# Long convolution of a hybrid encoder layer: short convolutions loaded two blocks ahead, the output transform split over two phases, the branch's first products beside the last spectra's turns

## The chip, the cores and the metric

The kernel runs on one core of one Trainium2 chip. Its time is the device time of the program in microseconds, the median of three runs.

## The reference, cut to what matters

One encoder layer, float32, 2048 positions of 1024 channels. An input projection feeds two mixers (a gated long convolution and a scan with a delta-rule state), their results are projected, gated, merged and normalised, and a feed-forward block follows. The change lies in the long-convolution mixer and in the first products of the merge behind it.

```python
def hyena_mixer(u, conv_w, conv_b, ..., skip):
    u = short_conv3(u, conv_w, conv_b)            # 3 taps over positions, 1536 channels
    v, x1, x2 = jnp.split(u, 3, axis=-1)          # 512 channels each
    h = hyena_filters(L, ...)
    z = x1 * long_conv(v, h[:, 0, 0], h[:, 0, 1], sk[0])    # by FFT of length 2L
    z = x2 * long_conv(z, h[:, 1, 0], h[:, 1, 1], sk[1])
    return z
...
y_h = hyena_mixer(u_h, ...) @ w_hy_out
y_r = rwkv_mixer(u_r, ...) @ w_rw_out
mix = (g_h * y_h + g_r * y_r) @ w_o
```

## The kernel before, in words

The 512 channels of the mixer are four blocks c = 0..3 of 128. For each block there are three rows of short convolution: v (row c), x1 (row 4 + c) and x2 (row 8 + c), each 128 channels by 2048 positions, computed in four blocks of 512 positions. The long convolutions are matrix products: a forward transform, a product with the filter's spectrum, an inverse transform. In order, the parts are:

- `shorts` (lines 1147 to 1183) is a generator; each `next` does one block of a row: SP loads block k+1 into one of two buffers `cu` (the inner `given`, line 1155, issued at the start of convolution k), ScalarE scales block k (line 1173), VectorE adds the two other taps (lines 1174 and 1179). The order of the rows is 0, 4, then 1, 5, 8, 2, 6, 9, 3, 7, 10, 11. Their results lie in two row buffers, X0 and X1. The row of block 0 is made in `open` (line 1115), near the end of the scan (`chain`), which ends with `output(*late.pop())` (line 1083) and leftover pieces of the scan and of the filters.
- `turn` (1267) transposes 4 x 128 positions on TensorE, and ScalarE copies them; `fwd` (1274) is a quarter of the forward transform, with two copies to `U` on ScalarE; `flips` (1284) gives a tile `V` and `piece(q)`, a 32x32-block transpose on VectorE (line 1289) of a quarter. The next step on TensorE reads all four quarters.
- `product` (1320), numbered 0 to 7, two for each channel block, has eight steps q. In each, TensorE makes `pz` from `V` (1295), VectorE multiplies it by the spectrum (1337 and 1338), TensorE makes `pz` of the spectrum two steps ahead (`load`, 1308, whose halves SP swaps with four small DMAs `rg<-rg`, line 1315) and turns the step before back (`back`, `pq`, 1328 and 1329). `extras[q]` are further works hung on step q: convolutions, pieces of transposes, turns. `self.upto` pulls pieces of the filter's transform (`pf`, `pg`), the filler of the stage; `goals` sets how far each step pulls. The spectra `Vf` are fetched by SP from DRAM (`given`, 1301).
- `inverse` (1353) is a quarter of the inverse transform (`po`). After an even product, the inner phase multiplies it by x1 into `z` (1443) and goes forward again; after an odd one, `finish` (1362) transposes it back to channels (`pv`, 1368, on TensorE), multiplies by x2 (the gate, 1370, VectorE) and stores the row to `yhd`.
- `ready` (1484) hangs on product 7 what the merge's first products need: eight weight tiles of the other branch, loaded and split into two parts each (ScalarE casts, VectorE subtracts, lines 197 and 198), gate values, the branch's rows `yrd` (`branch`, 1527). `right` (1521) is one such product, 12 matmuls of 128x256, with its gate on VectorE.

In the scan only TensorE's order is by hand, and a planner orders the other engines. In `hyena` the orders of TensorE, ScalarE, VectorE and SP are as written, so each engine and SP's queue take their work strictly in program order. The stage after product 2c, before the change, for c > 0, and the inner phase after it:

```python
piece(0); piece(1)
finish(c - 1, VQ2, x2, lambda q: piece(q + 1) if q in (1, 2) else None)
self.upto(min(self.pieces + 3, 32 * HT))
for q in range(6):
    if q < 4: p = inverse(VQ, q); tt(out=z[...], in0=p, in1=x1[...], op=ALU.mult)
    if q > 1: fwd(z, U, q - 2)
```

Of the kernel before, what the change touches and what calls it, by code (L numbers as in the profile page):

```python
# [189 lines left out]
class Layer:  # L190
# [432 lines left out]
    def chain(self):  # L623
# [3 lines left out]
        with tc.tile_pool(name="ch", bufs=1, reuse_waits="tile") as s, tc.tile_pool(name="chp", bufs=1, space=PSUM, reuse_waits="tile") as ps:  # L627
# [405 lines left out]
            with tc.manual_schedule(engines={mybir.EngineType.PE}):  # L1033
# [113 lines left out]
    def shorts(self):  # L1147
# [7 lines left out]
        def given(k):  # L1155
            ct, b = seq[k]
# [7 lines left out]
            return u  # L1164

        u = given(0)
        for k, (ct, b) in enumerate(seq):
            nxt = given(k + 1) if k + 1 < len(seq) else None
            if b == 0:
                o = self.cm.tile([P, L], F32, name="co", tag="X1" if ct == HT or ct >= 2 * HT else "X0")  # L1170
# [11 lines left out]
            u = nxt  # L1182
# [71 lines left out]
    def hyena(self):  # L1254
# [4 lines left out]
        with tc.tile_pool(name="hy", bufs=1, reuse_waits="tile") as s, tc.tile_pool(name="hyp", bufs=2, space=PSUM, reuse_waits="tile") as ps, \  # L1259
# [3 lines left out]
            def zt(name):  # L1263
                return s.tile([P, 16, P], F32, name=name, tag=name, bufs=1)

# [95 lines left out]

            def finish(c, Q, x2, beside):
                xv = x2.rearrange("p (a b) -> p b a", b=32)

                def back(q, v):
                    p = ps.tile([P, 4, P], F32, name="pv", tag="pq")
                    for j in range(4):
                        nc.tensor.transpose(p[:, j], v[:, j], self.ident)
                    w = xv[:, 8 * q:8 * q + 8]
                    tt(out=w, in0=p.rearrange("p a (b c) -> p (a b) c", b=2), in1=w, op=ALU.mult)  # L1370

                last = None
                for q in range(5):
                    if q < 4:
                        p = inverse(Q, q)
                        v = self.next("A")
                        nc.scalar.copy(v, p)
                    if q > 0:
                        back(q - 1, last)
                    beside(q)  # L1380
                    last = v
                if c == HT - 1:
                    self.yh = self.wp.tile([P, 2, TB], F32R, name="yh", tag="ev", bufs=2)
                    self.split(self.yh[:, 0], self.yh[:, 1], x2[:, 0:TB])
                nc.sync.dma_start(self.yhd[c], x2)
# [7 lines left out]
            def conv():  # L1393
                next(self.conv)
# [10 lines left out]
            x1, o = zt("x1"), self.convs.pop(HT)  # L1405
            Vz, piece = flips(U)
            for q in range(4):
# [3 lines left out]
                turn(o, x1, q)  # L1411
                self.upto(32 if q == 3 else min(32, self.pieces + 2))
            post, held = None, None
            for c in range(HT):
# [3 lines left out]
                if post:  # L1418
                    VQ2, piece2 = held
                    for q in range(4):  # L1420
# [3 lines left out]
                if more:  # L1424
                    for q in range(4, 8):
                        extras[q].append(conv)
# [3 lines left out]
                if post:  # L1430
                    x2 = self.convs.pop(2 * HT + c - 1)
                    piece(0)
                    piece(1)
                    finish(c - 1, VQ2, x2, lambda q: piece(q + 1) if q in (1, 2) else None)
# [373 lines left out]
```

## Time and profile before

| | us |
|---|---|
| median of three runs (4058.3 to 4072.2) | 4059.35 |
| the profiled execution | 4057.78 |
| its span, first to last instruction | 4056.0 |
| PE busy | 3851.7 |
| VectorE busy | 2350.6 |
| ScalarE busy | 1459.1 |

The profile is one execution. PE is TensorE's matmuls and PEld its weight loads; each float32 matmul shows as two records, a matmul of the rounded type as one. A busy PE at a granted clock of 0.5 does half the work. The long convolution lies between 1633 and 2205 us of the span; projection and scan lie before it, merge and feed-forward behind it.

### The profile page before, as it was taken

The page shows a single profiled execution, that of the slowest core. Times are in us where ns is not written, and L with a number is a line of the kernel's source. Part 1 is how long each engine was busy: PE and PEld are TensorE (multiplying, and loading weights), DVE is VectorE, ACT ScalarE, POOL GpSimd, SP SyncE. Part 2 cuts the span into 40 slices and gives each one's busy share as a digit, 9 for nine tenths or more (in the row PEclk, how much of TensorE's full clock was granted, in tenths as well). Part 3 has the DMA queues.
Part 4 walks back from the last instruction along what each step waited for, and adds up shares of the span by engine and source line. Part 5 has one row for each costly group of instructions (what it writes and reads, how often), then busy time and mean ns, then how long its engine had stood idle before and what let it go on. Part 6 is the DMA issues. An engine that isn't in the chain of part 4 may idle for free.

```text
span 4056.0 us, 64933 instructions
## 1 busy us (share of the span) xinstructions
PE 3851.7 (95%) x26152; PEld 3151.0 (78%) x26152; DVE 2350.6 (58%) x3734; ACT 1459.1 (36%) x2853; POOL 93.0 (2%) x139
## 2 busy tenths in 40 slices
PE   8999999899999998888987999999999999999998
PEld 6766557777777776788887899788888878888887
DVE  5456884665667774476665656544444464444444
ACT  3345662333335576555543323311111141111113
POOL 0000001111110100000000000000000000000000
PEclk9999999999999999899998999999999999999999
DMA  4566877677777766444454533411111133111111
GB/s 137 175 169 174 218 208 238 197 210 206 218 208 210 218 188 193 130 117 120 120 133 147 164 115 123 161 59 50 47 47 47 47 111 97 47 47 47 47 47 42
DMA packets 426564, 535.43 MB, mean 132 GB/s; under 512 B 137412, under 2 KB 305869, under 8 KB 423509
## 3 DMA queue, kind: packets, MB, share of 16 engines
q1 hardware_dynamic: 365847, 459.91, 38.7%
q10 hardware_dynamic: 54528, 54.59, 4.3%
q0 software_dynamic: 5888, 16.78, 1.6%
q8 instruction: 206, 3.38, 0.3%
q14 instruction: 95, 0.78, 0.1%
HBM read 369.52 MB, written 144.70 MB: 127 GB/s over the span
## 4 chain that ended last, share of the span: by engine, by line
PE 50%; DMA 3%; DVE 3%; ACT 2%; SPq 1%; issue 1%; DVEq 0%; ACTq 0%
PE pg L202 4%; PE pg L204 4%; PE pu L202 4%; PE pg L203 4%; PE pu L203 4%; PE pu L204 4%; PE pd L202 4%; PE pd L204 4%; PE pd L203 4%; PE pz L1295 2%; PE pm L204 1%; PE pm L202 1%; PE pm L203 1%; DMA cu<-ud 1%; PE po L202 1%; PE po L203 1%
## 5 line engine op out<-in xcount | busy, mean ns | idle before, releaser
L202 PE MATMUL acc<-xh,wh 128*128 128x512 f32 x1376 | 577.9, 420 | 10.4 <-ACT xh L197 10.4
L203 PE MATMUL acc<-xl,wh 128*128 128x512 f32 x1376 | 548.9, 399 | 9.4 <-DVE xl L198 9.4
L204 PE MATMUL acc<-xh,wl 128*128 128x512 f32 x1376 | 549.7, 399 | 0.5 <-DVE wl L198 0.5
L1745 DVE TENSOR_TENSOR acc<-pd,acc 128x1024 f32<-128x1024 f32 x320 | 387.5, 1221 | 70.8 <-PE pd L204 64.9
L197 ACT CAST fwh<-raw 128x1024 fp32r<-128x1024 f32 x132 | 138.5, 1049 | 704.2 <-PE pg L203 488.4
L202 PEld LDWEIGHTS acc<-xh,wh 128*128 128x128 f32 x1376 | 260.9, 190 | 123.5 <-issue 47.2
L1773 DVE TENSOR_TENSOR h<-pu,sg 128x512 f32<-128x512 f32 x88 | 60.8, 691 | 491.3 <-PE pu L204 485.3
L203 PEld LDWEIGHTS acc<-xl,wh 128*128 128x128 f32 x1376 | 261.4, 190 | 72.7 <-DVE xl L198 12.8
L204 PEld LDWEIGHTS acc<-xh,wl 128*128 128x128 f32 x1376 | 261.4, 190 | 63.8 <-DVE wl L198 1.0
L202 PE MATMUL pd<-fwh,hh 128*128 128x512 f32 x704 | 277.0, 394 | 1.8 <-DVE acc L1743 1.4
L202 PE MATMUL pg<-fxh,fwh 128*128 128x512 f32 x704 | 276.7, 393 | 0.2 <-DVE fxl L1660 0.2
L202 PE MATMUL pu<-fxh,fwh 128*128 128x512 f32 x704 | 276.3, 393 | 0.4 <-ACT fxh L1659 0.4
L204 PE MATMUL pg<-fxh,fwl 128*128 128x512 f32 x704 | 276.4, 393 | 0.0
L204 PE MATMUL pu<-fxh,fwl 128*128 128x512 f32 x704 | 276.1, 392 | 0.0
L203 PE MATMUL pu<-fxl,fwh 128*128 128x512 f32 x704 | 276.1, 392 | 0.0
L203 PE MATMUL pg<-fxl,fwh 128*128 128x512 f32 x704 | 275.9, 392 | 0.0
L204 PE MATMUL pd<-fwh,hl 128*128 128x512 f32 x704 | 275.1, 391 | 0.0
L203 PE MATMUL pd<-fwl,hh 128*128 128x512 f32 x704 | 274.5, 390 | 0.0
L198 DVE TENSOR_TENSOR fwl<-raw,fwh 128x1024 fp32r<-128x1024 f32 x132 | 161.1, 1221 | 165.8 <-ACT fwh L197 162.0
L198 DVE TENSOR_TENSOR wl<-wraw,wh 128x512 fp32r<-128x512 f32 (+1 forms) x217 | 169.7, 790 | 146.4 <-ACT wh L197 145.5
L197 ACT CAST wh<-wraw 128x512 fp32r<-128x512 f32 (+1 forms) x217 | 150.4, 704 | 232.0 <-PE acc L203 196.0
L202 PEld LDWEIGHTS pd<-fwh,hh 128*128 128x128 f32 x704 | 132.0, 187 | 40.6 <-DVE acc L1745 5.4
(288 smaller groups left out, 7545.9 us busy)
## 6 DMA issues: line engine op xcount, KB each, us to landing
wraw<-in_w_in SPq DMA_DIRECT2D x130, 512.0 KB, 4.6
ABp<-ABd SPq DMA_DIRECT2D x64, 512.0 KB, 5.6
raw<-in_fg SPq DMA_DIRECT2D x44, 512.0 KB, 3.4
raw<-in_fu SPq DMA_DIRECT2D x44, 512.0 KB, 3.5
raw<-in_fd SPq DMA_DIRECT2D x44, 512.0 KB, 3.5
ud<-ev ACTq DMA_DIRECT2D x84, 256.0 KB, 3.6
ABd<-AB SPq DMA_DIRECT2D x32, 512.0 KB, 5.3
gated<-ev SPq DMA_DIRECT2D x64, 256.0 KB, 3.4
```

Source lines behind the costliest of these rows:

```text
L197: nc.scalar.copy(hi, src)
L198: nc.vector.tensor_tensor(out=lo, in0=src, in1=hi.bitcast(F32), op=ALU.subtract)
L202: mm(ps, ah, bh, start=start, stop=False)
L203: mm(ps, ah, bl, start=False, stop=False)
L204: mm(ps, al, bh, start=False, stop=stop)
L1295: mm(p[:, j], Mc[:, 0 if 4 * q + j == 0 else 3], v[:, j], start=True, stop=True)
L1745: tt(out=acc[t], in0=pf, in1=acc[t], op=ALU.add)
L1773: tt(out=h, in0=put, in1=sg, op=ALU.mult)
```

## The change

- The loads of the short convolutions are issued two blocks ahead: two at the start, then that of block k+2 after convolution k, into the buffer that it has just read. The last row goes to X0 instead of X1.
- The row x1 of block 0 (four convolutions) is made at the end of the scan instead of beside the first turns. The other convolutions keep their number; within odd products they stand at steps 2, 4, 5, 6, 7, 7, and in even ones at 2, 3 (from c = 1 on) and 4 to 7. The last row moves from product 7 to product 6.
- The turns of x1 for the next block move from the last two steps of the odd product to the first four of the next even one; the pieces of transposes that hang on products move one step later.
- The output transform (`finish`) becomes `result`, `back` and `gate`. After an even product VectorE does its four pieces in a row; TensorE does the four inverses of the output and two backward turns. Gates and the other two turns go between the steps of the inner phase.
- Filler between an even product and the inner phase: six pieces for c = 0 and two otherwise, instead of three.
- The branch weights are loaded and split in product 6 instead of product 7. The branch's rows, its gate values and their `Tanh` come after the last block's transposes of `z`, into the row buffers `x1` and `z`, and three of the seven first products stand before product 7; four stand beside the last transposes. Product 7 has no extras. What `rest` loaded comes after product 7.

```diff
@@ chain
                 output(*late.pop())
+                self.x1 = self.short(HT)
@@ shorts
+        rows = {HT: "X1", 3 * HT - 1: "X0"}
...
-        u = given(0)
+        given(0)
+        given(1)
         for k, (ct, b) in enumerate(seq):
-            nxt = given(k + 1) if k + 1 < len(seq) else None
+            u = self.cus[k % 2]
...
-            u = nxt
+            given(k + 2)
             yield
@@ hyena
+            def result(Q, q):
+                p = inverse(Q, q)
+                v = self.next("AB"[q % 2])
+                nc.scalar.copy(v, p)
+                return v
+            def back(v):
+                p = ps.tile([P, 4, P], F32, name="pv", tag="pq")
+                for j in range(4):
+                    nc.tensor.transpose(p[:, j], v[:, j], self.ident)
+                return p
+            def gate(p, x2, q):
+                w = x2.rearrange("p (a b) -> p b a", b=32)[:, 8 * q:8 * q + 8]
+                tt(out=w, in0=p.rearrange("p a (b c) -> p (a b) c", b=2), in1=w, op=ALU.mult)
...
                 if q < 4:
                     turn(self.z0, z, q)
-                    conv()
...
-                turn(o, x1, q)
-                self.upto(32 if q == 3 else min(32, self.pieces + 2))
+                turn(self.x1, x1, q)
+                self.upto(32 if q == 3 else min(32, self.pieces + 3))
...
+                if c:
+                    VQ2, piece2 = held
+                    x1 = zt("x1")
                     for q in range(4):
-                        extras[q].append(lambda q=q: piece2(q))
-                    for q in (1, 3):
-                        extras[q].append(conv)
+                        extras[q].append(lambda q=q: turn(o1, x1, q))
+                        extras[q + 1].append(lambda q=q: piece2(q))
+                    extras[2].append(conv)
+                    extras[3].append(conv)
+                for q in range(4, 8):
+                    extras[q].append(conv)
+                if not more:
+                    self.ready(extras)
...
                 for q in range(4):
                     piece(q)
+                if c:
+                    x2 = self.convs.pop(2 * HT + c - 1)
+                    vs = [result(VQ2, q) for q in range(4)]
+                    ws = [back(vs[q]) for q in range(2)]
+                self.upto(min(self.pieces + 2 if c else self.pieces + 6, 32 * HT))
...
+                inner(0)
+                inner(1)
+                gated(0)
+                fwd(z, U, 0)
+                inner(2)
+                gated(1)
+                fwd(z, U, 1)
+                more_back(2)
+                inner(3)
+                gated(2)
+                fwd(z, U, 2)
+                more_back(3)
+                fwd(z, U, 3)
+                Vz, piece = flips(U)
+                gated(3)
+                if c:
+                    nc.sync.dma_start(self.yhd[c - 1], x2)
+                for q in range(4):
+                    piece(q)
...
+                else:
+                    self.inputs()
+                    for dt in range(3):
+                        self.right(ps, dt)
...
-                    for q in (1, 3, 4, 5, 6, 7):
+                    for q in (2, 4, 5, 6, 7, 7):
                         extras[q].append(conv)
...
+            self.outputs()
             for q in range(4):
                 piece(q)
-                self.right(ps, q)
+                self.right(ps, 3 + q)
+            for q in range(6):
+                if q < 4:
+                    vs.append(result(VQ, q))
+                if 0 < q < 5:
+                    ws.append(back(vs[q - 1]))
+                    gate(ws[q - 1], x2, q - 1)
@@ ready
+        extras[1].append(first)
+        for dt, q in enumerate((3, 4, 5, 5, 6, 6, 7, 7)):
+            extras[q].append(lambda dt=dt: weights(dt))
+    def inputs(self):
+        raw = self.spare_row("x1")...[:, 0:4 * TB]...
+        nc.sync.dma_start(raw, self.yrd[:, :, 0:TB].rearrange("c p t -> p c t"))
+        self.gates = self.spare_row("z")
+        for dt in range(7):
+            nc.sync.dma_start(self.gates[...], self.gated[8 + dt, :, 0:TB])
+        hl = [self.wp.tile([P, 4, TB], F32R, name="y", tag="wh", bufs=2) for k in range(2)]
+        self.split(*hl, raw)
+        g = self.gates[:, 0:14]
+        nc.scalar.activation(g, g, AF.Tanh, scale=0.5)
...
+    def outputs(self):
+        ...  the three row loads from yhd and the first weight of the other branch, as in rest before
```

## Rows read from the trace of the kernel before

**Rows 1.** From the page, the busy time of TensorE's matmuls: busy us, share of the span, number of instructions.

```profile
PE 3851.7 (95%) x26152; PEld 3151.0 (78%) x26152; DVE 2350.6 (58%) x3734; ACT 1459.1 (36%) x2853; POOL 93.0 (2%) x139
```

**Rows 2.** Busy time by engine in stages of the long convolution; columns: stretch in us, its length, then busy us and number of instructions of PE, PEld (weight loads), DVE (VectorE), ACT (ScalarE) and POOL, then the mean granted TensorE clock (1.00 is 2.4 GHz), the share of DMA and GB/s. The stages are: the end of the scan; the first turns; the transposes before product 0; product 0; after it; products 1 and 2; after 2; products 3 and 4; after 4; product 5; product 6; after 6 up to the last forward transform; the wait before product 7; product 7; the last transposes; the last inverse. The last line is a part of the stage after product 4, its four turns and forward transforms.

```profile
1597.00:1632.90 35.90, 25.27 (x200) 23.31 (x201) 10.99 (x28) 28.06 (x77) 0.00 (x0) 0.76 0.36 111
1632.90:1658.30 25.40, 13.16 (x82) 11.83 (x81) 8.17 (x11) 9.18 (x16) 0.00 (x0) 0.61 0.59 145
1658.30:1677.20 18.90, 18.27 (x137) 17.54 (x137) 12.62 (x10) 13.02 (x33) 0.00 (x0) 0.89 0.34 98
1677.20:1725.30 48.10, 42.83 (x354) 41.50 (x354) 21.03 (x32) 23.62 (x54) 0.00 (x0) 0.96 0.56 145
1725.30:1755.60 30.30, 22.66 (x220) 20.35 (x219) 20.20 (x14) 12.61 (x25) 0.00 (x0) 0.89 0.06 21
1755.60:1850.60 95.00, 89.48 (x765) 87.69 (x764) 64.53 (x83) 54.55 (x122) 0.00 (x0) 0.98 0.63 158
1850.60:1888.40 37.80, 30.95 (x315) 27.29 (x313) 26.18 (x19) 16.67 (x32) 0.00 (x0) 0.91 0.17 57
1888.40:1982.90 94.50, 89.41 (x764) 87.77 (x764) 64.60 (x83) 54.44 (x122) 0.00 (x0) 0.98 0.63 162
1982.90:2018.90 36.00, 30.64 (x314) 26.92 (x313) 26.07 (x19) 16.68 (x32) 0.00 (x0) 0.91 0.16 54
2018.90:2065.30 46.40, 45.75 (x403) 45.24 (x404) 33.15 (x42) 29.89 (x66) 0.00 (x0) 1.00 0.68 171
2065.30:2098.20 32.90, 31.77 (x284) 31.38 (x282) 22.56 (x28) 11.95 (x20) 0.00 (x0) 1.00 0.65 156
2098.20:2122.00 23.80, 19.10 (x209) 16.59 (x208) 15.30 (x12) 6.84 (x12) 0.00 (x0) 0.86 0.14 53
2122.00:2131.00 9.00, 0.03 (x1) 0.00 (x0) 8.29 (x4) 0.65 (x2) 0.00 (x0) 0.57 0.00 0
2131.00:2179.40 48.40, 36.43 (x241) 34.62 (x241) 22.00 (x34) 16.17 (x27) 0.00 (x0) 0.83 0.48 136
2179.40:2190.20 10.80, 5.81 (x50) 5.60 (x48) 9.64 (x8) 1.13 (x2) 0.00 (x0) 0.90 0.00 0
2190.20:2205.10 14.90, 14.60 (x128) 12.81 (x128) 6.21 (x8) 2.35 (x5) 0.00 (x0) 0.84 0.20 70
...
2009.50:2018.80 9.30, 8.94 (x81) 7.75 (x80) 8.59 (x4) 6.85 (x13) 0.00 (x0) 1.00 0.01 2
```

**Rows 3.** The timeline of the first turns, all engines; columns: start us, length us, engine, line, operation, out<-in, form, count, and in brackets the idle time before it with what ended it. SPq is SP's queue, which issues loads.

```profile
1634.48 3.65 SPq L1305 DMA_DIRECT2D Vf<-Hd  x8
...
1638.47 1.40 SPq L1163 DMA_DIRECT2D cu<-ud  x2
1647.17 0.81 ACT L1173 ACTIVATE cv<-cu,k_conv_b,k_conv_w 128x512 f32<-128x512 f32 x1 [11.83 <-DMA cu<-ud]
...
1648.51 0.79 PE L1280 MATMUL pfz<-z,Fz 64*128 64x128 f32 x2 [12.00 <-ACT U L1281]
```

**Rows 4.** Who waited for whom from 1632 to 2207 us: total us, number of waits, the longest one.

```profile
ACT cv L1173 <- DMA cu<-ud: 42.7, 14, 11.8
...
ACT co L1173 <- DMA cu<-ud: 17.5, 7, 5.1
...
PE pv L1368 <- DVE co L1370: 13.5, 6, 2.9
...
DVE rg L1338 <- DMA rg<-rg: 1.7, 1, 1.7
```

**Rows 5.** DMA issues of the same stretch: the short convolutions' loads with both edges inside the row; queue, count, KB each, median us from issue to landing.

```profile
cu<-ud SPq DMA_DIRECT2D x22, 257.0 KB, 5.3
```

**Rows 6.** Groups of instructions by line and form in the same stretch: line, engine, operation, out<-in, form, count, then busy us and mean ns of one, then idle us before them.

```profile
L1289 DVE STREAM_TRANSPOSE V<-U 128x1024 f32<-128x1024 f32 x64 | 140.9, 2229 | 29.2 <-ACT U L1281 24.0 <-ACT U L1330 5.1
...
L1179 DVE SCALAR_TENSOR_TENSOR co<-cu,k_conv_w,cv 128x512 f32<-128x512 f32 x28 | 31.3, 1116 | 1.0
...
L1174 DVE SCALAR_TENSOR_TENSOR cv<-cu,k_conv_w,cv 128x512 f32<-128x512 f32 x28 | 21.0, 751 | 67.7 <-ACT cv L1173 67.5
...
L1370 DVE TENSOR_TENSOR co<-pv,co 128x512 f32<-128x512 f32 x16 | 17.6, 1131 | 3.6 <-PE pv L1368 3.6
...
L198 DVE TENSOR_TENSOR wl<-wr,wh 128x512 fp32r<-128x512 f32 x8 | 5.5, 686 | 7.5 <-ACT wh L197 7.5
...
L198 DVE TENSOR_TENSOR y<-yraw,y 128x1024 fp32r<-128x1024 f32 x1 | 1.2, 1225 | 6.5 <-ACT y L197 6.5
```

**Rows 7.** The timeline of the stage after product 2 (columns as in rows 3): the first two transposed pieces, two backward turns, and the first inverse of the inner phase.

```profile
1854.31 4.29 DVE L1289 STREAM_TRANSPOSE V<-U 128x1024 f32<-128x1024 f32 x2
...
1855.14 0.66 PE L1368 MATMUL pv<-k_c_ident,rg 128*128 128x128 f32 x4
...
1862.74 1.08 PE L1368 MATMUL pv<-k_c_ident,rg 128*128 128x128 f32 x4 [2.42 <-DVE co L1370]
...
1868.14 1.09 PE L1358 MATMUL po<-V,Gc 128*64 128x128 f32 x16
```

**Rows 8.** The timeline of product 7, ScalarE (columns as in rows 3): the first cast of a branch weight, a convolution, the cast of the branch's rows.

```profile
2140.87 0.62 ACT L197 CAST wh<-wr 128x512 fp32r<-128x512 f32 x1 [4.73 <-DMA wr<-in_w_rw]
...
2147.56 0.81 ACT L1173 ACTIVATE co<-cu,k_conv_b,k_conv_w 128x512 f32<-128x512 f32 x1 [5.10 <-DMA cu<-ud]
...
2167.57 1.04 ACT L197 CAST y<-yraw 128x1024 fp32r<-128x1024 f32 x1 [7.39 <-DMA yraw<-yrd]
```

More of the change, by code (lines that the diff above doesn't have):

```diff
@@ L1359, in inverse @@
                 return p
[L1362 to L1385, printed above, removed]
+            def result(Q, q):
[11 more added lines that the diff above has]
+                tt(out=w, in0=p.rearrange("p a (b c) -> p (a b) c", b=2), in1=w, op=ALU.mult)
             def goals(i):
@@ L1417, in hyena @@
                 extras = {q: [] for q in range(8)}
-                if post:
+                if c:
                     VQ2, piece2 = held
+                    x1 = zt("x1")
                     for q in range(4):
-                        extras[q].append(lambda q=q: piece2(q))
-                    for q in (1, 3):
-                        extras[q].append(conv)
-                if more:
-                    for q in range(4, 8):
-                        extras[q].append(conv)
+                        extras[q].append(lambda q=q: turn(o1, x1, q))
[6 more added lines that the diff above has]
+                    self.ready(extras)
                 Q = self.pre()
@@ L1429, in hyena, with inner, gated, more_back @@
                 VQ, piece = flips(Q)
[L1430 to L1434, printed above, removed]
-                else:
-                    for q in range(4):
-                        piece(q)
-                self.upto(min(self.pieces + 3, 32 * HT))
-                z, U = zt("z"), self.pre()
-                for q in range(6):
-                    if q < 4:
-                        p = inverse(VQ, q)
-                        tt(out=z[:, 4 * q:4 * q + 4], in0=p, in1=x1[:, 4 * q:4 * q + 4], op=ALU.mult)
-                    if q > 1:
-                        fwd(z, U, q - 2)
-                Vz, piece = flips(U)
                 for q in range(4):
                     piece(q)
+                if c:
[3 more added lines that the diff above has]
+                self.upto(min(self.pieces + 2 if c else self.pieces + 6, 32 * HT))
+                z, U = zt("z"), self.pre()
+                def inner(q):
+                    p = inverse(VQ, q)
+                    tt(out=z[:, 4 * q:4 * q + 4], in0=p, in1=x1[:, 4 * q:4 * q + 4], op=ALU.mult)
+                def gated(q):
+                    if c:
+                        gate(ws[q], x2, q)
+                def more_back(q):
+                    if c:
+                        ws.append(back(vs[q]))
+                inner(0)
[13 more added lines that the diff above has]
+                gated(3)
+                if c:
+                    nc.sync.dma_start(self.yhd[c - 1], x2)
+                for q in range(4):
+                    piece(q)
+                Q2 = self.pre() if not more else None
                 if more:
@@ L1488, in first @@
             self.wr = [self.xp1.tile([P, 8, 4, P], F32R, name=f"w{n}", tag=f"x{n}", bufs=1) for n in "hl"]
-            self.gates = self.pre()
             self.wraws = [self.weights_raw("r", dt) for dt in range(2)]
-            for dt in range(7):
-                g = self.gates[:, 2 * dt:2 * dt + 2].rearrange("p a b -> p (a b)")
-                nc.sync.dma_start(g, self.gated[8 + dt, :, 0:TB])
         def weights(dt):
```

65 lines of the change are left out of this document (28 added, 37 removed).

## The prediction

> **What bounds the kernel now.** The page comes first: PE is busy for 95% of the span [rows 1], so what counts is where PE stands still or runs at half clock. Next a table by stage over the long convolution, the only part that the change touches [rows 2]. From 1632.9 to 2205.1 us PE works 490.9 of 572.2 us, so 81 us are idle there; ten stages have a mean granted clock of 0.91 or less, so PE spent parts of them at 1.2 instead of 2.4 GHz. The idle time has four homes. (a) The first turns, 1632.9 to 1658.3: 12.2 us, of which one wait takes 12.0. ScalarE sits in front of a short convolution until its load has landed, and the copy that frees PSUM for PE is queued behind it [rows 3]. (b) The stages of products 0 to 5 (from 1677.2, 1755.6, 1888.4 and 2018.9): 16.5 us. ScalarE waits for the loads `cu<-ud` 21 times from 1632 on, 60 us in all [rows 4]. (c) The stages after products 0, 2, 4 and 6 (from 1725.3, 1850.6, 1982.9 and 2098.2): 24.6 us, where PE waits for VectorE's transposes and for the gates between them [rows 4, 7]. (d) The last block: 9.0 us before product 7 and 12.0 in it (from 2122.0 and 2131.0). All later work starts when this ends, so a microsecond won here should be won at the end.
>
> **The sum** is made against the profiled execution, 4057.8 us; the median is 1.6 us above it.
>
> **1. First turns without convolutions: 14 us won.** The same four turns and forward transforms, with no convolution between them, took 9.3 us in a later block (the stage from 2009.5, [rows 2]), so 25.4 becomes 9.3: 16.1 won. In the next stage (0.89 granted) about 1 us comes back. The four convolutions now stand at the end of the scan. ScalarE is busy there for 28.1 of 35.9 us, so four ScalarE parts of 0.81 us [rows 2, 3] cost between nothing (they fit into its 7.8 idle us) and 12 us (the stall moves with them). I take 3.3, all four in series, because ScalarE is nearly full there, while their loads are now asked for two blocks ahead and no longer stand behind the eight `Vf` loads, as at 1638.5 [rows 3]. Those still have to land before the first `pz`; they were issued by 1638.1, the new turns end near 1642 and filter pieces follow, so I cost that at nothing; without that cover it would be some 3 us.
>
> **2. Loads two blocks ahead, products 0 to 5: 13 us won.** A block's load was issued at the start of the convolution before it, one step of about 5.4 us earlier (43 us of PE work in the eight steps of product 0, [rows 2]); it now has two steps less the convolution itself. Landing takes 5.3 us [rows 5], so one step was about too short, and two minus 2.7 us (0.81 + 0.75 + 1.12, [rows 3, 6]) is 8 us, enough unless SP is late. The most to win is the 16.5 idle us and about 5 at half clock, the least nothing. I take 60%: some gaps are VectorE's own (its transposes, beside which the turns now stand, since they move from the end of the odd product to the start of the even one), and those stay. The added wait is SP's: the load of block k+2 stands behind convolution k, so SP stops until VectorE has done it, and the swaps `rg<-rg` of the next step stand behind it. They are needed two steps later; I cost the wait at nothing while that slack lasts, some 4 us by estimate (two steps less a copy, four issues and a landing). With the slack gone, each hold counts in full.
>
> The Trainium skill, "DMA: Bandwidth & Descriptors", section "Anatomy of one DMA — SWDGE (gpsimd) path", gives a transfer on that path 2.0 us plus its bytes at 436 GB/s. An estimate by it for these 257 KB is 2.6 us: one step would have covered the load, this term would be nothing and the sum 36 instead of 49. No row here shows 2.6; the rows say 5.3, and 8.7 for the one behind the spectra, so the sum goes by them [rows 3, 5].
>
> **3. Output transform in two phases: 10.4 us won.** So far pieces of the transpose, gates and pieces in turn stand between the product and the next inverse. After product 2 this ran from 1854.3 to 1868.1, 13.8 us, with PE held by gates [rows 7]. Now four transposes of 2.23 us follow one another [rows 6], 8.9 us, and PE has the inverse (four times about 1 us) and two of the four backward turns beside them. The gates (1.13 us each) go beside the inner phase, which PE bounds. Off again go two backward turns in the inner phase (0.66 each, [rows 7]), one filter piece less as filler (0.9: 8 records, and product 6 shows 31.8 us for 284 of them, 0.112 each) and about 1.2 us at half clock, since PE still idles 2 to 3 us. Block 1: 4.9, plus 3.0 because the last convolution no longer holds the transposes (they began at 1854.3, while PE had left the product by 1850.6), less 3.4 for the charges: 4.5. Block 2's stage is 1.8 us shorter [rows 2], so 2.7. Block 3 idles least and has no late convolution ahead of it: 0.5. Block 0 has no output transform; three more filter pieces fill 2.7 of its 7.6 idle us and leave the product after it. Sum 10.4.
>
> **4. Product 6 takes the branch's weights and the last row's convolutions: 5.5 us lost.** It gets eight splits (VectorE 0.69 each), four convolutions (0.75 + 0.75 each) and the row's turns. VectorE's work becomes 34 us (22.6 + 5.5 + 6.0, [rows 2, 6]), bunched from step 2 on, and the stage lengthens from 32.9 to some 38. Bounds: 2 us, if that work packs without gaps, and 21.5, if all that product 7 loses for the same jobs comes along (48.4 - 26.9). I take a value near the low end: the first weights are fetched two steps before use, while in product 7 ScalarE stood 4.7 us before the first of them [rows 8].
>
> **5. From the last forward transform to the end of product 7: 12.4 us won.** Product 7 has 240 records left, 26.9 us at 0.112, and no load, convolution or weight in it: the waits of 4.7, 5.1 and 7.4 us all go [rows 8]. With about 1 us of latencies it takes 28 instead of 48.4. But ahead of it PE now has three first products, and they need the low half of the branch's rows, whose subtraction (1.23 us, [rows 6]) stands on VectorE behind four transposes. The products therefore don't fill the 9.0 us wait; they follow it: 0.6 for the last copy, 8.5 for the transposes (8.3 in the stage from 2122.0, [rows 2]), 1.2 for the subtraction, then 36 matmuls of 0.116 us (50 records in 5.81, the stage from 2179.4): 4.2 at full clock, and after 10 idle us I take 6.8. That makes 17.2 before product 7 instead of 9.0, and altogether 45.0 instead of 57.4. The seven gate loads, the row load and the `Tanh` lie beside the transposes; without that cover up to the 7.4 us that ScalarE waited for the row load would come on top.
>
> **6. Tail: 4.5 us won.** Four first products lie beside the last transposes as before. Three (12 matmuls each, 4.2 us) are gone from the final inverse's 14.9 us [rows 2]. The loads that `rest` issued now follow product 7, with the transposes as cover.
>
> Sum: 14 + 13 + 10.4 - 5.5 + 12.4 + 4.5 = 48.8, so 4057.8 - 48.8 + 1.6 = 4011 us, faster.
>
> **Rivals.** *Loads no earlier.* SP issues them late rather than early, behind its swaps and `Vf` loads, and more distance in program order buys no time. Term 2 goes, and 3.7 us of term 3 (the 3.0 of block 1 and 0.7 of block 2): 32.1 are left, 4027 us. For it: the 8.7 us load behind the spectra; against it: a median of 5.3 that two steps cover. By the figure of the Trainium skill's DMA page, too, term 2 would go. Chance 0.13. *Product 6 jams as product 7 did*: term 4 becomes 21.5, 4027 us, chance 0.12. For it: the cast that waited for weights; against it: they are fetched earlier. *The first stall only moves*, into the scan's end, and the change doesn't do what it says there: the 3.3 becomes 12, 4019 us, chance 0.10. *SP's new wait*, the slower side: it holds the swaps beyond their slack in every step with a convolution. Some 36 such steps would have to lose 1.4 us each to eat up the 49 us; at 2 us each the time is 4011 + 72 = 4083. It decides once a swap lands over 4 us later than now. Against it: VectorE waited for a swap once, 1.7 us [rows 4]. Chance 0.05. The forecast has 0.60.
>
> **Range and chances.** The good ends together (17, 20 and 15 for terms 1 to 3, 2 lost in product 6, 3 more in term 5) give 3989; 4040 takes in the first three rivals and one of them with a weak term 1 or 5. A measurement of this kernel can tell about 0.5%, 20 us, from no change. Faster by more: the forecast and most of the first three rivals, 0.84. Within: 0.11. Slower: 0.05.
>
> **What would show it.** Right: no wait for `cu` on ScalarE over 3 us after 1640; first turns near 10 us; four `V` transposes back to back after each even product, with the gates among the `z` products; the three first products after the `y` subtraction; product 7 in 28 us. Wrong: VectorE waiting for swaps; product 6 over 45 us; a new PE gap near 12 us in the scan's last steps.

## The result: 25 us won, half of the forecast

Timed on one chip the changed kernel took 4038.73 us (median) against 4061.65 for the kernel before, ratio 0.9938 (95% interval 0.9915 to 0.9962), some 25 us by the ratio and 23 between the medians. Timed again on another chip: 0.9948 (0.9936 to 0.9961), 21 us. The forecast was 4011 us. The profiled execution took 4032.94 us, its span is 24.9 us below that of before. The page's line on busy time:

```profile
PE 3842.6 (95%) x26152; PEld 3144.0 (78%) x26152; DVE 2353.7 (58%) x3734; ACT 1458.5 (36%) x2851; POOL 93.0 (2%) x139
```

Against [rows 1] the same 26152 matmuls take 9 us less (less half clock); the rest of the gain is idle time of PE.

Up to 1633 us both kernels do the same but for four convolutions, and executions differ there by several us either way; so stages are read from there on. The stages after the change, columns as in [rows 2]: the first turns with the transposes; everything from product 0 to the end of product 5; of that, products 2 and 4 alone; product 6; from there to product 7; product 7; the rest up to the merge's first product with the output branch's weights.

```profile
1632.80:1660.70 27.90, 24.99 (x219) 23.30 (x218) 13.42 (x12) 20.08 (x47) 0.00 (x0) 1.00 0.63 161
1660.70:2043.00 382.30, 348.18 (x3110) 335.07 (x3109) 255.70 (x288) 206.82 (x443) 0.00 (x0) 0.96 0.48 128
1778.70:1830.30 51.60, 45.56 (x380) 44.70 (x379) 34.41 (x45) 27.69 (x61) 0.00 (x0) 0.93 0.57 146
1911.40:1963.60 52.20, 46.17 (x382) 45.27 (x380) 34.17 (x45) 27.20 (x60) 0.00 (x0) 0.93 0.56 147
2043.00:2094.00 51.00, 38.12 (x298) 36.81 (x297) 35.25 (x48) 21.65 (x37) 0.00 (x0) 0.92 0.67 178
2094.00:2132.60 38.60, 25.46 (x246) 23.29 (x246) 26.40 (x20) 10.23 (x15) 0.00 (x0) 0.79 0.21 65
2132.60:2160.40 27.80, 27.22 (x244) 27.06 (x243) 10.73 (x17) 7.61 (x13) 0.00 (x0) 1.00 0.27 68
2160.40:2186.20 25.80, 15.05 (x140) 13.27 (x138) 15.54 (x15) 4.48 (x9) 0.00 (x0) 0.91 0.36 119
```

Set beside before (sums of [rows 2], with the same ends). In the forecast's column the 0.5 us that term 3 gave to block 3 stands with product 7, and the 14 of term 1 are 17.1 in this stretch less 3.3 at the scan's end:

| stretch | before | forecast | after | won |
|---|---|---|---|---|
| first turns to product 0 | 44.3 | 14 won | 27.9 | 16.4 |
| products 0 to 5 and the stages between | 388.1 | 22.9 won (13 + 9.9) | 382.3 | **5.8** |
| product 6 | 32.9 | 5.5 lost | 51.0 | **-18.1** |
| from there to the end of product 7 | 81.4 | 12.9 won | 66.4 | 15.0 |
| the rest of the span | 1876.4 | 4.5 won | 1870.7 | 5.7 |

Two rows make the whole shortfall. The last row is weaker than it looks: of its 5.7 us only 1.2 lie ahead of the merge's first product with the output branch's weights (27.0 before, 25.8 now); the other 4.5 lie behind it, in 1845 us whose code the diff leaves as it was.

Who waits there (columns as in [rows 4], from 1632 to 2187 us):

```profile
...
PE pf L1221 <- DVE rg L1239: 21.8, 5, 6.3
...
ACT co L1177 <- DMA cu<-ud: 12.8, 4, 4.3
...
ACT wh L197 <- DMA wr<-in_w_rw: 10.8, 5, 5.1
ACT cv L1177 <- DMA cu<-ud: 10.5, 5, 3.1
...
DVE rg L1344 <- DMA rg<-rg: 8.3, 5, 2.2
```

ScalarE's wait for the short convolutions' loads fell from 60 to 23 us, as meant. But a wait that was not there before now stands first among PE's: PE for the filter's multiply `rg`. Three of its five times, 14.2 of the 21.8 us, are at the start of an even product. The timeline of the first of them shows the chain (columns as in [rows 3]):

```profile
1772.70 7.16 SPq L1321 DMA_DIRECT2D rg<-rg  x4
1772.97 1.12 DVE L1183 SCALAR_TENSOR_TENSOR co<-cu,k_conv_w,cv 128x512 f32<-128x512 f32 x1
...
1778.37 0.81 ACT L1177 ACTIVATE co<-cu,k_conv_b,k_conv_w 128x512 f32<-128x512 f32 x1 [0.63 <-DMA cu<-ud]
...
1779.97 0.52 SPq L1167 DMA_DIRECT2D cu<-ud  x1
...
1783.45 0.82 ACT L1177 ACTIVATE co<-cu,k_conv_b,k_conv_w 128x512 f32<-128x512 f32 x1 [4.27 <-DMA cu<-ud]
...
1785.88 0.69 DVE L1343 TENSOR_TENSOR rg<-pz,rg 128x512 f32<-128x512 f32 x1
...
1787.08 0.68 DVE L1239 TENSOR_TENSOR rg<-pg,rg 128x512 f32<-128x512 f32 x1
...
1787.91 2.04 PE L1221 MATMUL pf<-rg,Fc 128*128 128x128 f32 x8 [5.43 <-DVE rg L1239]
```

Odd products now hold their six convolutions at steps 2, 4, 5, 6, 7 and 7. The load for the second one at step 7 waits for step 6's convolution (done at 1774.1) and then for SP, which is at that step's swaps until 1779.9: they took 7.2 us, and of these the trace puts 3.6 down to a wait for a store of the filter (`Hd<-cu`). The load lands some 3.4 us after its issue. ScalarE's half of the convolution, VectorE's half, VectorE's products for the next step, the filter multiply and PE stand in line behind it. PE idles 5.4, 4.7 and 4.1 us at the starts of products 2, 4 and 6, and its granted clock is 1.2 GHz for 6.8, 6.8 and 3.4 us there.

### The profile page after: what moved, and what is told of

The parts are those of the page before. It is cut to its first block, busy times and chain, and to the rows that moved or that the text cites. A ratio compares the mean times of both kernels' runs of the same rounds, so it can differ in the third digit from the quotient of the medians.

```text
span 4031.1 us, 64982 instructions
## 1 busy us (share of the span) xinstructions
PE 3842.6 (95%) x26152; PEld 3144.0 (78%) x26152; DVE 2353.7 (58%) x3734; ACT 1458.5 (36%) x2851; POOL 93.0 (2%) x139
## 3 DMA queue, kind: packets, MB, share of 16 engines
q1 hardware_dynamic: 365847, 459.91, 38.7%
## 5 line engine op out<-in xcount | busy, mean ns | idle before, releaser
L203 PEld LDWEIGHTS acc<-xl,wh 128*128 128x128 f32 x1376 | 262.9, 191 | 74.5 <-DVE xl L198 14.2
```

Of the source, the lines that this page charges most:

```text
L203: mm(ps, ah, bl, start=False, stop=False)
```

## The experiments

All are timed in five rounds; a ratio is to the kernel before on the same chip, and 0.001 is about 4 us.

**One convolution per step.**

```
-                    for q in (2, 4, 5, 6, 7, 7):
+                    for q in (2, 3, 4, 5, 6, 7):
                         extras[q].append(conv)
```

> The changed kernel with one edit: in products 1, 3 and 5 the six convolutions stand one to a step (steps 2 to 7) instead of at 2, 4, 5, 6, 7, 7. Theory A (the pair at step 7): the second convolution of the pair needs a load that is issued only behind the convolution of step 6, it lands too late, ScalarE and VectorE stand, and PE then idles 5.4, 4.7 and 4.1 us at the start of products 2, 4 and 6 and runs at half clock for 6.8, 6.8 and 3.4 us after. Without the pair the three gaps go and the kernel is 16 to 22 us faster than the changed one, 41 to 47 us faster than the kernel before. Theory B (SP's queue): loads are late because SP is held at the swaps, so one convolution per step only moves the wait to another step; at most 6 us won against the changed kernel. Theory C (VectorE too full: transposed pieces at steps 1 to 4 beside convolutions): new gaps in steps 3 and 4, 0 to 8 us won.

Measured 0.9903 (0.9888 to 0.9918), 39 us under the kernel before, 14 to 18 under the changed one. The control on a later chip:

> One convolution per step again, as control on the same chip: ratio to the kernel before 0.989 to 0.992.

It gave 0.9910 (0.9887 to 0.9933). Products 0 to 5, products 2 and 4, and product 6 of the first:

```profile
1661.40:2031.30 369.90, 342.19 (x3110) 329.44 (x3109) 256.34 (x290) 207.59 (x444) 0.00 (x0) 0.98 0.50 133
1781.30:1825.90 44.60, 43.37 (x382) 42.53 (x380) 32.70 (x43) 26.73 (x59) 0.00 (x0) 1.00 0.62 158
1906.90:1952.30 45.40, 43.25 (x382) 42.51 (x380) 32.72 (x43) 26.81 (x59) 0.00 (x0) 1.00 0.62 162
2031.30:2077.60 46.30, 36.50 (x298) 35.14 (x296) 34.58 (x46) 21.22 (x36) 0.00 (x0) 0.95 0.72 190
```

The three gaps are gone, the clock stays at 1.00 in products 2 and 4, and 12.4 us come back up to product 6 and 4.7 in it. The other traces agree: products 0 to 5 took 382.3 us in the changed kernel's second trace, and 369.6 to 372.6 in seven with one convolution per step and the same filler and output transform (an eighth, with 388.2, has the long stretch at half clock shown at the end). By the two second traces 9.7 us come back up to product 6 and 5.4 in it. Theory A holds in the changed kernel.

**The loads on another queue**, pair kept: `nc.gpsimd.dma_start` in place of `nc.sync.dma_start` for `cu<-ud`.

> The changed kernel with one edit: the loads of the short convolutions are issued on POOL's queue instead of SP's, so that they no longer stand behind swaps and spectra; the pair of convolutions at step 7 stays. Theory B: the issue comes within a microsecond of the convolution that frees the buffer, the waits for the loads on ScalarE fall from 23 us to under 8, the three PE gaps of 5.4, 4.7 and 4.1 us fall under 1.5 us, 16 to 22 us won against the changed kernel. Theory A: the load of the pair's second convolution can start some 6 us earlier at best (at 1774 instead of 1780) but still has only one step, so the gaps fall by 2 to 4 us each and don't vanish; 6 to 12 us won. If POOL's loads land later than SP's 5.3 us, the kernel becomes slower instead.

Measured 0.9942 (0.9921 to 0.9962), no better than the changed kernel. The pair's second load, its convolution and PE:

```profile
1779.73 0.55 POOL L1167 DMA_DIRECT2D cu<-ud  x1 [4.81 <-ACT cu L1223]
...
1785.78 0.81 ACT L1177 ACTIVATE co<-cu,k_conv_b,k_conv_w 128x512 f32<-128x512 f32 x1 [2.22 <-DMA cu<-ud]
...
1790.24 1.27 PE L1221 MATMUL pf<-rg,Fc 128*128 128x128 f32 x8 [2.65 <-DVE rg L1239]
```

(This execution stands 5.2 us later than the changed kernel's at product 2.) The load goes out half a microsecond behind its convolution instead of 5.9, but takes 6 us to land instead of 3.4. The gaps become 2.7, 1.9 and 1.1 us: each falls by 2.7 to 3.0, A's figure. But products 0 to 5 take 369.1 us and product 6 47.8, together 16.4 less than in the changed kernel, B's figure; the stages after products 2 and 4 shorten too, from 35.5 and 34.8 to 32.7 and 32.9. So both are at work: the pair leaves one step, and SP spends it. Why the median gained nothing is not settled: in this execution the first turns start 7 us later, but executions differ there by that much without any edit. The Trainium skill, "DMA: Bandwidth & Descriptors", section "Issuing engines are not separate DMA queues", says that transfers from several engines share the same DMA engines and that only issue time is saved; the one load shown agrees, issued 5.4 us earlier behind its convolution and 2.6 us longer in landing.

**The pair alone**, in the kernel before with loads two blocks ahead: steps 1, 4, 5, 6, 7, 7 for 1, 3, 4, 5, 6, 7.

> The kernel before with the loads two blocks ahead and one more edit: in the odd products the convolutions stand at steps 1, 4, 5, 6, 7, 7 instead of 1, 3, 4, 5, 6, 7. If the pair at step 7 is by itself the cause: PE gaps of 3 to 6 us at the end of products 1, 3 and 5 or the start of the next, 8 to 17 us slower than without the pair (ratio to the kernel before 0.997 to 0.999 instead of 0.9949). If it takes the rest of the change to make the load late: within 4 us.

Measured 0.9994 (0.9981 to 1.0006), 18 us slower than without the pair. But the experiment does not show what it was meant to:

```profile
1786.55 1.09 PE L1273 MATMUL ph<-k_c_ident,co 128*128 128x128 f32 x8 [3.29 <-DVE co L1181]
```

The 3.3 us gaps (one in each odd product) are the turns of the x1 row, which in that kernel stand at steps 6 and 7 and wait for the row's fourth convolution; the edit moved it from step 5 to step 6. The gaps that answer to the pair are 1.2 and 2.0 us, and its second convolution waited 1.6 us for its load. So the pair's price depends on how soon its second load goes out, and the 5 us or so for each pair are its price in the changed kernel. That the rest of the change makes SP fuller is argued from these traces, not tested.

**Single parts of the change in the kernel before.** Only the loads two blocks ahead:

> The kernel before with one part of the change alone: the loads of the short convolutions are asked for two blocks ahead, issued behind the convolution that frees the buffer; everything else as before, convolutions at steps 1, 3 to 7 of odd products and 1, 3 to 7 of even ones. The prediction's terms 2 and the 3.7 us of term 3: 13 to 17 us faster than the kernel before, and the 11.8 us wait in the first turns may shrink too. The rival that loads come no earlier: within 4 us of the kernel before.

0.9949 (0.9934 to 0.9964), 21 us. Only the first x1 row's convolutions moved to the scan's end:

> The kernel before with one part of the change alone: the four convolutions of the first x1 row stand at the end of the scan instead of between the first turns, with the loads one block ahead as before. Term 1 of the prediction: the first turns take 9 to 11 instead of 25.4 us, the scan's end gets 0 to 4 us longer, 11 to 17 us faster than the kernel before. Rival (the stall only moves): the scan's end gets some 12 us longer and at most 5 us are won.

0.9958 (0.9945 to 0.9972), 17 us. First turns with transposes, products 0 to 5, and product 7 with loads two ahead; then the first two stretches with the moved convolutions:

```profile
1631.80:1672.00 40.20, 29.44 (x218) 27.56 (x217) 20.65 (x21) 21.92 (x49) 0.00 (x0) 0.79 0.54 138
1672.00:2048.80 376.80, 345.49 (x3127) 332.35 (x3127) 257.48 (x291) 209.55 (x448) 0.00 (x0) 0.97 0.49 131
2115.10:2157.90 42.80, 34.43 (x242) 33.31 (x243) 22.14 (x34) 16.45 (x27) 0.00 (x0) 0.85 0.50 148
```

```profile
1630.10:1656.50 26.40, 25.00 (x218) 23.18 (x217) 13.16 (x11) 19.66 (x46) 0.00 (x0) 1.00 0.68 170
1656.50:2044.80 388.30, 350.36 (x3126) 335.27 (x3126) 255.73 (x291) 208.61 (x448) 0.00 (x0) 0.97 0.48 129
```

Loads two ahead win 11.3 us in products 0 to 5 (388.1 before); the rest of their 21 lies in the first turns and in product 7, which the full change clears in other ways. The moved convolutions win 17.9 us in the first turns and nothing after.

**The branch's weights in product 6.** In the changed kernel two weights share a step from step 5 on, with loads two deep:

```profile
2087.32 0.62 ACT L197 CAST wh<-wr 128x512 fp32r<-128x512 f32 x1 [5.06 <-DMA wr<-in_w_rw]
```

```profile
2090.24 0.77 PE L1334 MATMUL pq<-rg,Mc 128*128 128x128 f32 x2 [4.75 <-DVE rg L1343]
```

First, spread from step 1 on (their first loads in step 0; splits in steps 1 to 7, two in step 7):

> The changed kernel with one edit: in product 6 the branch's weights are split one to a step from step 1 on (two in step 7), their first loads asked for in step 0, instead of at steps 3, 4, 5, 5, 6, 6, 7, 7. Theory: where two stand in one step, the second waits for a load that the first one's buffer let out (ScalarE waited 3.5 and 5.1 us), and that makes the PE gap of 4.75 us at the end of product 6 and the small ones ahead of it; spread out, product 6 takes 34 to 37 instead of 41 us and the kernel is 5 to 9 us faster than the changed one. Rival: VectorE's sheer work in product 6 (30.6 us) sets its length; then the gaps only move, 0 to 3 us won.

0.9949 (0.9932 to 0.9966), no gain. In its trace product 6 takes 44.1 us, 6.9 less, but the stretch behind it 51.5 instead of 38.6, because PE runs at 1.2 GHz for 37.5 us on end there:

```profile
2103.60:2141.10 37.50, 26.92 (x159) 24.04 (x160) 17.70 (x15) 7.43 (x10) 0.00 (x0) 0.50 0.21 67
```

That execution was the slowest of its six, so for the time the experiment is inconclusive. For product 6 it is not: with all eight weights still in it, spreading them alone took 6.9 us off. Then four of the weights moved to steps 0 to 3 of product 7, on top of one convolution per step, twice; and six of the eight left out:

> On top of one convolution per step: only four of the branch's eight weights are split in product 6 (one in each of steps 4 to 7), the other four in steps 0 to 3 of product 7. Theory: the weights, two to a step behind loads two deep, are what makes product 6 46.3 us long there (32.9 before the change), and its gap of 5.1 us at the end; product 6 becomes 36 to 40 us, product 7 28 to 31 instead of 27.8, 5 to 9 us won against one convolution per step alone. Rival: the last row's convolutions and turns make product 6 long; then it stays over 43 us, and the time is within 2 us or slower.

> One convolution per step with four weights in product 7, again, on the same chip as the control. If the end follows product 6: 4 to 9 us faster than the control. Rival: within 2 us.

> One convolution per step, and six of the branch's eight weights are left out: only two are loaded and split (steps 3 and 4 of product 6), and the first products and the merge use these two in turn for all eight. It leaves out work to price it. Theory (the weights lengthen product 6 by waiting for their loads, and the end follows): product 6 36 to 39 instead of 46.3 us, 6 to 12 us faster than with all weights. Rival (what is won there is given back behind it, to the transposes and the rows' load): within 3 us of it.

Measured 0.9906 (0.9892 to 0.9919) and 0.9913 (0.9887 to 0.9939) for the split, 0.9895 (0.9878 to 0.9912) with six left out, against 0.9903 and 0.9910 for all eight in product 6. In the traces product 6 is the same in all three, here the split's, with product 7 behind it:

```profile
2037.30:2075.20 37.90, 34.41 (x298) 33.38 (x296) 29.58 (x39) 17.73 (x31) 0.00 (x0) 1.00 0.75 194
...
2115.60:2143.40 27.80, 27.22 (x244) 27.06 (x244) 13.13 (x21) 9.68 (x17) 0.00 (x0) 1.00 0.33 86
```

46.3 becomes 37.9 us: weights bunched behind their loads cost 8.4 us of product 6, and four of them cost nothing in product 7. The 6.9 us that spreading alone gave, pair and all, say that most of it is the waiting, not the work. That the end follows is not shown: some 1.7 us come back in the stretch behind, and executions of one kernel scatter too far (4002 to 4036 us in the second timing) for the rest to show.

**The output transform in its old form**, on top of one convolution per step (pieces, results, backward turns and gates interleaved again for rows 0 to 2):

> One convolution per step, with the output transform of rows 0 to 2 in its old form: pieces, results, backward turns and gates interleaved between the product and the inner phase, as before the change; the pieces' filler as in the changed kernel. The prediction put 7.7 us on this for blocks 1 to 3 (4.5, 2.7, 0.5), of which 3.0 came from the late convolution. By theory A (stage lengths of the traces: 37.7 became 34.6 and 35.9 became 34.4) undoing it costs 3 to 6 us; if the four transposes in a row only traded one VectorE wait for another, undoing it costs nothing, within 2 us.

0.9923 (0.9910 to 0.9935), by the ratios 5 to 8 us slower than the two timings of the two-phase form, whose intervals it overlaps. The stages after products 2 and 4 take 36.2 and 36.7 us where one convolution per step has 34.5 and 34.3, and 36.6 and 35.3 in its second trace; the one from product 6 to product 7 takes 40.9 for 38.7 and 39.3. So the old form costs something, between 1 and 4 us in the two stages.

**Then filler ahead of the transposes**, on top of the last kernel of this section (e9); in block 0 one more piece stands behind the second inverse:

```
                 VQ, piece = flips(Q)
+                self.upto(min(self.pieces + 2, 32 * HT))
                 for q in range(4):
                     piece(q)
...
-                self.upto(min(self.pieces + 2 if c else self.pieces + 6, 32 * HT))
+                self.upto(min(self.pieces + 3, 32 * HT))
```

> As e9, and two filter pieces issued ahead of the four transposes, so that VectorE's multiply for them does not stand behind the transposes, and three behind (in block 0 one more after the second inverse). Theory: in the stages after products 0, 2 and 4 PE waits 6.3, 4.6 and 4.6 us because the filler it has left needs a multiply queued behind 8.3 us of transposes; with the multiplies ahead the waits fall to some 4, 3 and 3 us and the half-clock stretch after them shortens: 4 to 9 us faster than e9. Rival: the multiplies push the transposes back by as much, 0 to 2 us.

0.9867 (0.9853 to 0.9882), 4000.71 us, the fastest of all, 10 us under e9. What it acts on, in the changed kernel after products 0 and 2:

```profile
1703.94 8.32 DVE L1295 STREAM_TRANSPOSE V<-U 128x1024 f32<-128x1024 f32 x4
1712.18 1.24 DVE L1239 TENSOR_TENSOR rg<-pg,rg 128x512 f32<-128x512 f32 x2
...
1712.87 3.78 PE L1221 MATMUL pf<-rg,Fc 128*128 128x128 f32 x16 [6.34 <-DVE rg L1239]
```

```profile
1834.10 8.45 DVE L1295 STREAM_TRANSPOSE V<-U 128x1024 f32<-128x1024 f32 x4
1842.43 0.68 DVE L1239 TENSOR_TENSOR rg<-pg,rg 128x512 f32<-128x512 f32 x1
1842.70 3.68 PE L1364 MATMUL po<-V,Gc 128*64 128x128 f32 x32 [4.60 <-DVE V L1295]
```

The filler's multiply is queued behind four transposes. In e11 the 4.6 us waits become 2.0, and the stages after products 2 and 4 run at full clock throughout, here the first of them. After product 0 nothing changed: the wait of 6.2 us only stands before the inverse now.

```profile
1830.70:1862.60 31.90, 28.30 (x313) 25.19 (x312) 27.05 (x20) 16.17 (x31) 0.00 (x0) 1.00 0.26 86
```

For c > 0 the edit also asks for five pieces between the product and the inner phase instead of two, so it doesn't separate where the filler stands from how much of it there is.

**The last block's ends.** The merge's cast waits until the last row's store has landed, since that row moved to the buffer over which the cast's target lies. The layout was turned round (`"lw", "lb", "acc2", "acc3"` for `"acc2", "acc3", "lw", "lb"`):

> On top of one convolution per step: the order in which the merge's fixed buffers are laid out is turned round, so that the cast branch rows (acc2, acc3) no longer lie on the memory of the last output row. Theory: in the changed kernel the last row moved to the buffer X0, over which acc2 and acc3 lie; the cast of the merge's rows therefore waits until the row's store has been read out (ScalarE waits 4.2 us, till the moment the store lands) and PE idles 6.0 us before the merge's first product. With the other layout that gap falls under 2 us and the kernel is 4 to 8 us faster than with one convolution per step alone. Rival: the cast waits for something else (its loads, the splits queued behind the last gates); then the gap stays and the time is within 2 us.

0.9903 (0.9889 to 0.9916), nothing won. The gap fell as expected, and the next one took its place:

```profile
2186.24 0.58 PE L202 MATMUL pm<-y,whh 128*128 128x256 f32 x1 [6.00 <-ACT y L197]
```

```profile
2165.38 0.38 PE L202 MATMUL pm<-y,whh 128*128 128x256 f32 x1 [1.68 <-ACT y L197]
...
2172.99 0.58 PE L202 MATMUL pm<-y,whh 128*128 128x256 f32 x1 [3.65 <-DVE h L1579]
```

(The first row is the changed kernel's.) Then the branch's rows loaded earlier, their split behind the first transpose:

> On top of one convolution per step: the branch's rows are loaded behind the last z product instead of behind the last output store, and their split stands behind the first of the four transposes instead of behind all four. Theory: the three first products start some 3.5 us earlier, beside the transposes; what then sets the start of product 7 is the last transpose, pushed back by the 1.2 us subtraction; product 7 starts 2 to 5 us earlier, 2 to 5 us won. Rival: the load takes the time (ScalarE waited 5.6 us for it), the split holds the transposes behind it and product 7 starts no earlier or later: 0 to 3 us lost.

0.9887 (0.9872 to 0.9901), 4012.10 us, some 6 us by the ratio, though the intervals overlap; its stage shows 5.0. In the changed kernel, and here:

```profile
2117.28 8.33 DVE L1295 STREAM_TRANSPOSE V<-U 128x1024 f32<-128x1024 f32 x4 [1.11 <-ACT U L1287]
...
2123.96 0.58 PE L202 MATMUL pr<-y,wh 128*128 128x256 f32 x1 [7.34 <-ACT y L197]
2125.50 1.20 DVE L198 TENSOR_TENSOR y<-x,y 128x1024 fp32r<-128x1024 f32 x1
```

```profile
2102.33 0.39 PE L202 MATMUL pr<-y,wh 128*128 128x256 f32 x1 [1.62 <-ACT y L197]
...
2111.23 0.94 PE L1301 MATMUL pz<-V,Mc 128*128 128x128 f32 x6 [0.56 <-DVE V L1295]
```

The three first products now lie beside the transposes, and the last transpose sets product 7's start, 5.0 us earlier. Both together with the split weights (e9), and the changed kernel again:

> One convolution per step, with four of the weights in product 7 and the branch's rows loaded and split earlier, together. Theory: the two shorten different stretches (product 6; the stretch from the last forward transform to product 7), so they add: product 6 takes 38 us, from the last inverse's start to product 7 about 34 to 36 us, product 7 28 us, 40 to 50 us faster than the kernel before by the ratio 0.988 to 0.9855. Rival: what product 6 gives is taken back behind it (with the split alone the stretch after it grew by 1.7 us and the median did not move): ratio 0.989 to 0.990.

> The changed kernel again, unchanged, on the same chip as the experiments: ratio to the kernel before 0.992 to 0.9955. Theory A then has one convolution per step 12 to 20 us faster than it.

0.9891 (0.9879 to 0.9904) and 0.9948 (0.9936 to 0.9961). In its trace e9 has every stage as expected (37.9, 35.2 and 28.1 us), but its ratio is that of e7: as with the split alone, the median does not show what product 6 gains.

## Why the prediction was wrong in size

**1, first turns: right.** 16.4 us came back where the working had 17.1 (16.1 + 1). The 3.3 us charged to the scan's end did not come: that stage takes 35.8 us, 35.9 before, so the rival that the first stall only moves is out.

**2, loads two blocks ahead: the step that failed.** It gave each load "two steps less the convolution itself" and so "8 us, enough unless SP is late". That is the distance where one convolution stands in a step. The diff puts two into step 7 of every odd product, and there the distance is one step less a convolution, with SP at the swaps. The text did not look at that place. The part alone won 11.3 us in its stretch, near the forecast 13, so loads did come earlier. In the changed kernel the pair takes 12.4 us of it back, and 4.7 us of product 6 (9.7 and 5.4 by the second traces). The rival of SP's new wait had the right queue but not the place: it priced a small loss in some 36 steps, and the loss came in three steps.

**3, output transform: right in kind, too large.** Four transposes in a row took 8.3 to 8.5 us for 8.9 forecast, but PE idles 4.6 us there, not "2 to 3", and 6.3 in block 0, where the three more filler pieces were to fill it: two of their multiplies wait behind the transposes. Undoing the part for rows 0 to 2 cost 5 to 8 us by the ratios, and 1 to 4 us in the two stages of blocks 1 and 2, where 7.2 were forecast.

**4, product 6: mis-sized.** 18.1 us lost for 5.5. Of that, 4.7 is the pair of product 5, which idles PE in product 6's first step, and 8.4 the weights bunched behind their loads; what is left, 5.0 with four weights in it, is near the forecast. "The first weights are fetched two steps before use" holds for the first two only; from the third on a weight's load waits for the split two weights earlier. The rival that product 6 jams (21.5) came near: 18.1, or 13.4 without the pair.

**5: right.** From product 6 to the end of product 7 15.0 us were won for 12.9; product 7 takes 27.8 us, 28 forecast, and it starts 16.0 us after the last forward transform, 17.2 forecast, with the subtraction behind the transposes as said. (The working's own parts, 28 and 17.2, give 45.2 and not 45.0, which changes nothing.)

**6, tail: the number is right, but not by the working.** In the stages that it speaks of 1.2 us were won for 4.5, since a new 6.0 us wait stands there, which the prediction did not have; taking it away moved nothing in the time. The other 4.5 us of the row lie behind the merge's first product. There the four traces with the old tail took 1848.7 to 1855.5 us and the fourteen with the new one 1844.2 to 1850.8, so part of it is likely real; why stays open.

By the first trace of each kernel the shortfall adds up: 17.1 for the pair, 7.9 for the weights against what term 4 allowed, 4.7 in what is left of terms 2 and 3 (22.9 forecast, 18.2 with one convolution per step), less 5.7 that terms 1, 5 and 6 won beyond the forecast: 24.0, and 48.8 - 24.9 is 23.9. It is that close by luck: the second traces have 15.1 for the pair, and 4.5 of what was won beyond the product stages is not explained. The times alone show 14 to 18 us for the pair. That the weights' share reaches the end stays open. Of the signs named, product 6 over 45 us came true, and a `cu` wait over 3 us; VectorE's waits for swaps grew from 1.7 to 8.3 us, none over 2.2.

## What to carry to other kernels

A buffer that is asked for two uses ahead has as much time as lies between the use that frees it and the use that needs it: work that out at the place where uses stand closest, not on average. Jobs that each wait for a load belong one to a step; two in a step made the whole queue behind the second wait here, three times. Filler only fills as far as all that it needs stands ahead of the long instructions it is to cover: here its multiplies stood behind them, and PE waited 4.6 to 6.3 us.

## What the runs showed of the hardware

A transfer's time from issue to landing was not the same in every kernel: the same 257 KB loads had a median of 5.3 us before [rows 5], 3.4 us in the changed kernel and 3.8 us on POOL's queue (5.2 for the loads of 256.5 KB there):

```profile
cu<-ud SPq DMA_DIRECT2D x19, 257.0 KB, 3.4
```

```profile
cu<-ud POOLq DMA_DIRECT2D x19, 257.0 KB, 3.8
```

So 5.3 was no property of the transfer, and the sum used it as one. What sets the time was not tested. The Trainium skill, "DMA: Bandwidth & Descriptors", section "Anatomy of one DMA — SWDGE (gpsimd) path", gave the estimate of 2.6 us; none of the three medians agrees, not even that on POOL's queue, whose path the section describes.

A wait of the same length can cost very different amounts of clock. The stage after product 2, with one convolution per step and in the kernel with six weights left out, which differ only later; the third row is the second kernel's stretch at half clock:

```profile
1825.90:1860.40 34.50, 28.77 (x305) 25.73 (x304) 26.32 (x19) 15.98 (x30) 0.00 (x0) 0.95 0.24 78
```

```profile
1816.70:1867.60 50.90, 44.16 (x305) 39.35 (x304) 26.12 (x19) 16.44 (x30) 0.00 (x0) 0.62 0.17 54
```

```profile
1829.10:1870.10 41.00, 39.89 (x227) 35.70 (x228) 17.25 (x15) 11.73 (x20) 0.00 (x0) 0.50 0.07 26
```

In both PE stood 4.6 us before the same inverse. In one the granted clock was 1.2 GHz for 3.4 us around it, in the other for 41 us, of which PE was busy for 39.9, and 16 us were lost. This is one source of the scatter between executions, and differences under 8 us were hard to time here.
